# Moving a small tile out of a pool, one load ahead of another, and a last slot in column halves

## The chip, the cores and the metric

The kernel runs on one core of a Trainium2 chip. The metric is the device time of one execution in microseconds (us). Before the change three runs took 1791.95, 1792.40 and 1792.44 us, a median of 1792.4. A run of this kernel can be told from another at about 0.2%, some 3.6 us.

## The reference

Four layers of a streaming encoder on 256 tokens of width 2048, in fp32. Cut to what matters here:

```python
for i in range(DEPTH):                    # 4 layers; kinds 0, 1, 2, 0
    h = rms_norm(x, norm_g[i])
    z = h @ w_in                          # 2048 -> 5632 (kind 0) or 7168 columns (+12 in kind 1)
    mix_out = mixer(z[..., :n_mix])       # gated MLP, forgetting attention or differential attention
    kv = rms_norm(mem, mem_norm_g) @ w_mem_kv[i]      # 2048 -> 1024, 256 memory rows
    mem_out = memory_attention(rms_norm(mem_q), rms_norm(kv[..., :512]), kv[..., 512:])
    branch = concat([mix_out, mem_out], -1) * silu(gate)
    x = x + branch @ w_out[i]             # 2048 -> 2048
```

## The kernel before

**Products.** Nearly all of TensorE's work is the big products: the memory projections of all four layers, the input projections and the output projections. A product is cut into chunks of 512 output columns, a chunk into 8 slots, and a slot takes 256 of the 2048 summed rows: two depth tiles (`kk`) of 128. There are 592 slots in all. Each fp32 operand is split into a rounded part and the rest (`hi` and `lo`), and a product of two operands is three matmuls: hi x hi, lo x hi and hi x lo. So a slot is 2 (`kk`) x 2 (token tiles `t`) x 3 = 12 matmuls of 128x128 stationary against 128x512 moving (lines 170 to 172 in `slot_product`). The stationary tile is a slice of the activations (`bh`/`bl` or `xh`/`xl`, 128 tokens of one depth tile), the moving one a slice of the weights (`whi`/`wlo`). In the last slot of a chunk the first token tile goes first.

**Which activations.** `bh0` to `bh7` with `bl0` to `bl7` hold the memory's transposed rows first (64 slots, before the layers) and later the branch (the output projections, 128 slots). `xh0` to `xh7` with `xl0` to `xl7` hold the token rows for the input projections (400 slots). The number is the slot's share of the depth, `kp`.

**Where the tiles lie.** A tile's place in a partition comes from its pool: pools stand one behind another, and in a pool tiles stand in the order in which they are first asked for. The weight pool `wpool` has only tiles of 4096 bytes. The pool `act` follows: `bh0, bl0, bh1, bl1` (2048 bytes each, asked for in the start-up code), then the three buffers of the row factors `r` (`row_factors`, line 369: 16 columns of which 2 are used, 64 bytes each, 192 bytes in all), then all the other parts `b` and `x`, each 2048 bytes. Within a multiple of 512 bytes the built program has all weight tiles and the parts b0 and b1 at 416, and the parts b2 to b7 and x0 to x7 at 96. A slice of a tile starts a multiple of 512 bytes behind the tile's start. So in the slots of b0 and b1 (48 of the 592) the stationary and the moving operand lie at the same place within 512 bytes, and in the other 544 they lie 192 bytes apart.

**Order of the work.** The order on TensorE, ScalarE (ACT), VectorE (DVE) and SyncE (SP) is that of the code. Between two slots (`between_slots`) the running tasks (norms, attention, gates, residuals) each issue one step, small fp32 products and transposes among them (of PE's 8290 matmul records 7104 are those of the slots and 520 are transposes), and the weights of the slot four ahead are split: ACT copies `raw` to `whi` (line 119), DVE subtracts for `wlo` (line 120). SP loads `raw` up to eight slots ahead.

**Start.** Line 243 loads the first half of the memory tile on ACT's queue, line 244 the norm weights `gk` behind it, and SP's queue loads the first weight tile and the other half. The first split (`scaled_part`, line 205) needs both loads of ACT's queue.

**End.** `residual_task` adds the old rows to an output chunk (line 788, one DVE addition for each token tile). In the last layer the sum goes straight to the output, the first token tile from SP's queue, the second from ACT's (line 790).

Of the kernel before, what the change touches and what calls it, by code (L numbers as in the profile page):

```python
# [9 lines left out]
F32 = mybir.dt.float32  # L10
# [9 lines left out]
P = 128  # L20
D = 2048
S = 256
DEPTH = 4
KT = D // P
CW = 512
# [3 lines left out]
NEG = -1e30  # L29
BIG = 3.0e38  # L30
BIAS_PITCH = 512
ROW_PAD = 16
BIAS_COPIES = 16
RAW_BUFS = 4
PART_BUFS = 4
# [8 lines left out]
def trunk_kernel(  # L44
# [23 lines left out]
    nc = tc.nc  # L68
# [3 lines left out]
    act = ctx.enter_context(tc.tile_pool(name="act", bufs=1))  # L72
    heads = ctx.enter_context(tc.tile_pool(name="heads", bufs=2))
    tmp = ctx.enter_context(tc.tile_pool(name="tmp", bufs=2))
    small = ctx.enter_context(tc.tile_pool(name="small", bufs=32))
# [7 lines left out]
    def piece_sequence():  # L83
        seq = []
        for i in range(1, DEPTH):
            for n in (1, 0):
                seq.append((w_kv[i, n], range(8)))
        for i in range(DEPTH):
            src = (w_a[i // 3], w_b, w_c)[i % 3]
            for n in range(11 if i % 3 == 0 else 14):  # L90
                seq.append((src[n], range(8)))
            for n in range(4):
                seq.append((w_o[i, n], range(8) if n else (0, 1, 2, 3, 6, 7, 4, 5)))
        first = [(w_kv[0, n], kp) for kp in range(8) for n in (1, 0)]
        return first + [(src, kp) for src, order in seq for kp in order]

    pieces = piece_sequence()
# [33 lines left out]
    def tick():  # L131
        for gen in list(tasks):
            if next(gen, tasks) is tasks:
                tasks.remove(gen)
        tasks.extend(fresh)
        fresh.clear()

    def run_late():
        todo = list(late)
        late.clear()  # L140
        for fn in todo:
            fn()

    def between_slots():
        tick()
        split_until(state["slot"] + PART_BUFS)
        load_until(state["slot"] + PART_BUFS + RAW_BUFS)
        run_late()

    def slot_product(acc, parts_of, first, last):  # L150
        between_slots()
        slot = state["slot"]
        kp = pieces[slot][1]
        guard = 0
        while parts_of(kp) is None:
            assert (tasks or fresh) and guard < 100
            tick()
            run_late()
            guard += 1
        xh, xl = parts_of(kp)  # L160
        hi, lo = parts.pop(slot)
        order = [(kk, t) for kk in range(2) for t in range(2)]
        if last:
            order.sort(key=lambda o: o[1])
        for kk, t in order:
            begin, end = first and kk == 0, last and kk == 1
            wh = hi[:, kk * CW : (kk + 1) * CW]
            wl = lo[:, kk * CW : (kk + 1) * CW]
            c = slice(kk * S + t * P, kk * S + (t + 1) * P)
            nc.tensor.matmul(acc[t], xh[:, c], wh, start=begin, stop=False)  # L170
            nc.tensor.matmul(acc[t], xh[:, c], wl, start=False, stop=False)  # L171
            nc.tensor.matmul(acc[t], xl[:, c], wh, start=False, stop=end)  # L172
        state["slot"] += 1
# [4 lines left out]
    def chunk_product(parts_of):  # L178
        acc = new_acc()
        for n in range(8):  # L180
            slot_product(acc, parts_of, n == 0, n == 7)
        return acc

    def pair_product(parts_of):
        accs = [new_acc(), new_acc()]
        for n in range(16):
            slot_product(accs[n % 2], parts_of, n < 2, n >= 14)
        return accs


    gk = const.tile([P, 5 * KT], F32, name="gk")
# [6 lines left out]
    def new_parts(kind, kp):  # L198
        hi = act.tile([P, 2 * S], F32R, tag=f"{kind}h{kp}", name=f"{kind}h{kp}")
        lo = act.tile([P, 2 * S], F32R, tag=f"{kind}l{kp}", name=f"{kind}l{kp}")  # L200
        return hi, lo
# [8 lines left out]
    def scaled_split(hi, lo, src, gcol):  # L210
        for kk in range(2):
            c = slice(kk * S, (kk + 1) * S)
            scaled_part(hi[:, c], lo[:, c], src[:, c], gcol + kk)
# [26 lines left out]
    raw = tmp.tile([P, 2 * S], F32, tag="xo", name="xraw", bufs=4)  # L240
    m_hi, m_lo = new_parts("b", 0)
    bparts[0] = (m_hi, m_lo)
    nc.scalar.dma_start(raw[:, :S], mem_t[0, :, :S])
    nc.scalar.dma_start(gk, gk_in)
    nc.sync.dma_start(w_raw[:, :CW], pieces[0][0][0, :, :CW])
    nc.sync.dma_start(raw[:, S:], mem_t[0, :, S:])
    nc.sync.dma_start(w_raw[:, CW:], pieces[0][0][0, :, CW:])
# [5 lines left out]
    for k in range(2):  # L253
        c, w = slice(k * S, (k + 1) * S), slice(k * CW, (k + 1) * CW)
# [21 lines left out]
    def finish_rms(ss, r):  # L276
        nc.vector.tensor_reduce(r, ss, AX.X, ALU.add)
        rsqrt_mean(r, r, 2, D)
# [88 lines left out]
    mk_d = [dram.tile([P, 4 * S], F32, name=f"mk_d{i}") for i in range(DEPTH)]  # L367
    mv_d = [dram.tile([P, 2 * CW], F32, name=f"mv_d{i}") for i in range(DEPTH)]
    def row_factors(name):
        return act.tile([P, ROW_PAD], F32, tag="r", name=name, bufs=3)[:, :2]  # L370

    r_mem, r_x = row_factors("r_mem"), row_factors("r_x")

    def delayed(n, gen):
# [7 lines left out]
    for i in range(DEPTH):  # L382
        acc = first_accs[0] if i == 0 else chunk_product(lambda kp: bparts[kp])
# [7 lines left out]
        acc = first_accs[1] if i == 0 else chunk_product(lambda kp: bparts[kp])  # L391
# [381 lines left out]
    def old_rows(i, n):  # L773
        res = []
        for t in range(2):
            rows, cols = slice(t * P, (t + 1) * P), slice(n * CW, (n + 1) * CW)
            xo = tmp.tile([P, CW], F32, tag="xo", name="xo", bufs=4)
            nc.sync.dma_start(xo, x[rows, cols] if i == 0 else x_d[i - 1][n][t])
            res.append(xo)
        return res  # L780

    def residual_task(acc, i, n, xo, ss, r_next):
        last = i == DEPTH - 1
        xn = []
        for t in range(2):
            rows, cols = slice(t * P, (t + 1) * P), slice(n * CW, (n + 1) * CW)
            xt = tmp.tile([P, CW], F32, tag="tb", name="xn", bufs=4)
            nc.vector.tensor_add(xt, acc[t], xo[t])  # L788
            if last:
                (nc.sync, nc.scalar)[t].dma_start(out[rows, cols], xt)  # L790
                continue
            nc.gpsimd.dma_start(x_d[i][n][t], xt)  # L792
            xn.append(xt)
        if last:
            return

        def squares():
            for t in range(2):
                sq = tmp.tile([P, CW], F32, tag="sq", name="sq", bufs=2)
                nc.scalar.activation(sq, xn[t], AF.Square, accum_out=ss[:, t, n : n + 1])  # L800

        late.append(squares)
        for jj in range(2):
            yield
            kp = 2 * n + jj
            tb = ps_t.tile([P, 4, P], F32, tag="t", name="tb")
            for kk in range(2):
                for t in range(2):
                    f = (2 * jj + kk) * P
                    nc.tensor.transpose(tb[:, 2 * kk + t, :], xn[t][:, f : f + P], ident)  # L810
            hi, lo = new_parts("x", kp)
            scaled_split(hi, lo, tb.rearrange("p a b -> p (a b)"), KT * (i + 1) + 2 * kp)
            xparts[kp] = (hi, lo)
        if n == 3:
            finish_rms(ss, r_next)

    for i in range(DEPTH):
# [9 lines left out]
        def product():  # L827
            return chunk_product(lambda kp: xparts[kp])
# [26 lines left out]
        if kind == 0:  # L855
# [3 lines left out]
            for c in range(3):  # L859
                acc = product()  # L860
# [9 lines left out]
            for c in range(3):  # L870
                acc = product()
# [6 lines left out]
        else:  # L878
# [10 lines left out]
            for c in range(3):  # L889
                ready = []  # L890
                acc = product()
                qt = heads.tile([P, 4, S], F32, tag="qT", name="qt")
                spawn(norm_task(acc, r_x, qgains[:, gq : gq + 1], width, qt))
                acc = product()
# [11 lines left out]
                acc = product()  # L906
# [22 lines left out]
            for c in range(3):  # L929
                gate(c)  # L930

        r_next = row_factors("r_x")
        ss = small.tile([P, 2, 4], F32, tag="ss", name="ss", bufs=2)
        for n in range(4):
            xo = old_rows(i, n)
            acc = chunk_product(lambda kp: bnext[kp])
            spawn(residual_task(acc, i, n, xo, ss, r_next))
# [89 lines left out]
```

## Time and profile before

| | before |
|---|---|
| runs (3) | 1791.95 to 1792.44 us, median 1792.4 |
| profiled execution | 1792.09 us |
| its span, first to last instruction | 1790.3 us |
| TensorE (PE) busy | 1782.3 us, 8290 matmul records |
| weight loads (PEld) busy | 1461.0 us |
| VectorE busy | 1021.0 us |
| ScalarE busy | 905.1 us |
| granted TensorE clock, mean | 1.000 |

A busy matmul record overlaps the next one: of a stream of equal matmuls the time is read from the distance between starts, not from the records' length. The profiled execution is 1.8 us longer than its span, and 0.3 us under the median of the runs.

### The profile page before, as it was taken

What the parts mean: (1) busy time and instruction counts of PE and PEld (TensorE: products, weight loads), DVE (VectorE), ACT (ScalarE), POOL (GpSimd) and SP (SyncE); (2) the same over time, 40 slices, a digit from 0 to 9 for tenths busy, and PEclk for the clock granted to TensorE, in tenths of its full rate; (3) what the DMA queues carried; (4) which work ended last, traced back from release to release, by engine and by line L of the source; (5) the groups of instructions that cost most, each with busy time, mean ns of one, the idle gap of its engine ahead of it and who ended that gap; (6) DMA issues with size and microseconds to landing.
All of it is one profiled execution on the core that took longest, in us unless ns stands there. A gap on an engine that the chain in (4) does not pass through costs nothing.

```text
span 1790.3 us, 22226 instructions
## 1 busy us (share of the span) xinstructions
PE 1782.3 (100%) x8290; PEld 1461.0 (82%) x8290; DVE 1021.0 (57%) x1431; ACT 905.1 (51%) x1273; POOL 115.5 (6%) x138
## 2 busy tenths in 40 slices
PE   9999999999999999999999999999999999999999
PEld 6788888888888888888888887878788888888887
DVE  5555557555555555555555555666565556755453
ACT  6555545544555544545445555565554544554432
POOL 0110100000001101010000110102000000100000
PEclk9999999999999999999999999999999999999999
DMA  8767765555676554455767655454546766455564
GB/s 297 268 229 259 245 225 169 188 178 183 225 227 197 173 193 153 160 182 170 206 221 228 198 174 171 156 167 169 172 157 219 230 217 229 157 172 180 188 219 158
DMA packets 103452, 353.91 MB, mean 198 GB/s; under 512 B 12028, under 2 KB 12340, under 8 KB 103216
## 3 DMA queue, kind: packets, MB, share of 16 engines
q1 hardware_dynamic: 97200, 332.84, 56.2%
q0 software_dynamic: 5280, 18.44, 3.3%
q8 instruction: 65, 1.06, 0.3%
q10 hardware_dynamic: 864, 1.22, 0.2%
q14 instruction: 43, 0.35, 0.1%
HBM read 339.55 MB, written 12.89 MB: 197 GB/s over the span
## 4 chain that ended last, share of the span: by engine, by line
PE 96%; DMA 2%; ACT 0%; DVE 0%; issue 0%; POOL 0%; SPq 0%; ACTq 0%; DVEq 0%; POOLq 0%
PE acc L170 30%; PE acc L172 29%; PE acc L171 29%; PE tb L562 2%; PE tb L357 1%; PE tb L571 1%; PE tb L622 1%; PE s L470 1%; PE s L512 1%; DMA row<-in_mem_dram 1%; PE sv L688 1%; DMA raw<-in_w_kv_dram 1%; PE tb L810 1%; PE s L487 0%; DMA mv_d<-mvv 0%; DMA xraw<-in_mem_t_dram 0%
## 5 line engine op out<-in xcount | busy, mean ns | idle before, releaser
L120 DVE TENSOR_TENSOR wlo<-raw,whi 128x1024 fp32r<-128x1024 f32 x591 | 722.8, 1224 | 604.9 <-ACT whi L119 600.7
L119 ACT CAST whi<-raw 128x1024 fp32r<-128x1024 f32 x591 | 619.3, 1049 | 523.9 <-PE acc L172 470.1
L170 PE MATMUL acc<-whi,xh 128*128 128x512 f32 x1600 | 646.3, 404 | 0.0
L172 PE MATMUL acc<-whi,xl 128*128 128x512 f32 x1600 | 628.2, 393 | 0.0
L171 PE MATMUL acc<-wlo,xh 128*128 128x512 f32 x1600 | 623.8, 390 | 0.0
L172 PEld LDWEIGHTS acc<-whi,xl 128*128 128x128 f32 x1600 | 300.4, 188 | 68.8
L170 PEld LDWEIGHTS acc<-whi,xh 128*128 128x128 f32 x1600 | 300.9, 188 | 63.9 <-issue 3.2
L171 PEld LDWEIGHTS acc<-wlo,xh 128*128 128x128 f32 x1600 | 301.0, 188 | 61.3
L170 PE MATMUL acc<-whi,bh 128*128 128x512 f32 x768 | 304.3, 396 | 1.3 <-ACT whi L256 0.7
L171 PE MATMUL acc<-wlo,bh 128*128 128x512 f32 x768 | 300.4, 391 | 0.8 <-DVE wlo L120 0.6
L172 PE MATMUL acc<-whi,bl 128*128 128x512 f32 x768 | 300.2, 391 | 0.0
L172 PEld LDWEIGHTS acc<-whi,bl 128*128 128x128 f32 x768 | 144.2, 188 | 32.6 <-DVE bl L206 0.4
L170 PEld LDWEIGHTS acc<-whi,bh 128*128 128x128 f32 x768 | 144.3, 188 | 32.2 <-ACT whi L256 1.3
L171 PEld LDWEIGHTS acc<-wlo,bh 128*128 128x128 f32 x768 | 144.4, 188 | 32.0 <-DVE wlo L120 1.7
L575 ACT COPY pt<-tb 128x256 f32<-128x256 f32 (+1 forms) x80 | 27.2, 341 | 127.4 <-PE tb L571 127.3
L320 POOL TENSOR_TENSOR sc<-sc,expo 128x8 f32<-128x8 f32 (+1 forms) x23 | 55.9, 2431 | 540.3 <-DVE sc L319 474.0
L206 DVE SCALAR_TENSOR_TENSOR xl<-tb,gk,xh 128x256 fp32r<-128x256 f32 x48 | 23.2, 484 | 29.6 <-ACT xh L205 29.5
L205 ACT ACTIVATE xh<-tb,gk 128x256 fp32r<-128x256 f32 x48 | 22.8, 475 | 33.0 <-PE tb L810 19.7
L626 ACT CAST bh<-tb 128x512 fp32r<-128x512 f32 x26 | 15.3, 588 | 47.4 <-PE tb L622 47.4
L792 POOL DMA_DIRECT2D x_d<-xn x24 | 13.2, 549 | 314.1 <-DVE xn L788 313.3
L475 DVE TENSOR_REDUCE st<-s 128x1 f32<-128x256 f32 x32 | 13.6, 425 | 32.2 <-PE s L470 32.2
L585 DVE TENSOR_SCALAR mo<-tb,st 128x128 f32<-128x128 f32 x56 | 19.4, 346 | 19.3 <-ACT pt L575 16.5
(160 smaller groups left out, 959.6 us busy)
## 6 DMA issues: line engine op xcount, KB each, us to landing
raw<-in_w_a_dram SPq DMA_DIRECT2D x176, 512.0 KB, 3.3
raw<-in_w_o_dram SPq DMA_DIRECT2D x128, 512.0 KB, 3.6
raw<-in_w_b_dram SPq DMA_DIRECT2D x112, 512.0 KB, 3.3
raw<-in_w_c_dram SPq DMA_DIRECT2D x112, 512.0 KB, 3.2
raw<-in_w_kv_dram SPq DMA_DIRECT2D x63, 512.0 KB, 4.3
x_d<-xn POOLq DMA_DIRECT2D x24, 256.0 KB, 6.1
xo<-x_d SPq DMA_DIRECT2D x24, 256.0 KB, 5.5
lnp<-in_ln_dram SPq DMA_DIRECT2D x12, 256.0 KB, 6.1
```

Source lines behind the costliest of these rows:

```text
L119: nc.scalar.copy(hi, raw)
L120: nc.vector.tensor_sub(lo, raw, hi.bitcast(F32))
L170: nc.tensor.matmul(acc[t], xh[:, c], wh, start=begin, stop=False)
L171: nc.tensor.matmul(acc[t], xh[:, c], wl, start=False, stop=False)
L172: nc.tensor.matmul(acc[t], xl[:, c], wh, start=False, stop=end)
L205: nc.scalar.activation(hi, src, AF.Copy, scale=g)
L206: nc.vector.scalar_tensor_tensor(lo, src, g, hi.bitcast(F32), ALU.mult, ALU.subtract)
L320: nc.gpsimd.tensor_tensor(sc[:, :, :n], sc[:, :, :n], expo.rearrange("p (a b) -> p a b", a=2)[:, :, :n], ALU.pow,)
L357: nc.tensor.transpose(tb[:, i, :], qn[t][:, i * P : (i + 1) * P], ident)
L562: nc.tensor.matmul(av, pt[:, j * P : (j + 1) * P], vv[:, j, f], start=(j == 0), stop=(j == tiles(t) - 1),)
L575: nc.scalar.copy(pt[:, : nk * P], tb[:, : nk * P])
L585: nc.vector.tensor_scalar(mo[t][:, f], av, done_st[:, 2:3], None, ALU.mult)
```

## The change

Four edits. The row factors are no longer tiles of the `act` pool but of `small`, the last of the pools there, with 2 columns; with that every part `b` and `x` lies at 416 within 512 bytes, as the weight tiles do, and everything that stands behind the old `r` tiles moves down by 192 bytes (the constants, among them `ident`, stay). The load of `gk` is issued ahead of that of the memory tile. The very last slot is issued by `final_slot`: 24 matmuls of 256 moving columns, token tile by token tile, left column half first. And in the last layer the residual addition and the store of each token tile are made in two column halves, the left one stored from SP's queue, the right one from ACT's.

```diff
--- before.py
+++ after.py
@@ -29,7 +29,6 @@
 NEG = -1e30
 BIG = 3.0e38
 BIAS_PITCH = 512
-ROW_PAD = 16
 BIAS_COPIES = 16
 RAW_BUFS = 4
 PART_BUFS = 4
@@ -147,6 +146,19 @@
         load_until(state["slot"] + PART_BUFS + RAW_BUFS)
         run_late()
 
+    def final_slot(acc, xh, xl, hi, lo):
+        half = CW // 2
+        for t in range(2):
+            for a in (0, half):
+                for kk in range(2):
+                    w = slice(kk * CW + a, kk * CW + a + half)
+                    c = slice(kk * S + t * P, kk * S + (t + 1) * P)
+                    for n, (xx, ww) in enumerate(((xh, hi), (xh, lo), (xl, hi))):
+                        nc.tensor.matmul(
+                            acc[t][:, a : a + half], xx[:, c], ww[:, w],
+                            start=False, stop=(a > 0 and kk == 1 and n == 2),
+                        )
+
     def slot_product(acc, parts_of, first, last):
         between_slots()
         slot = state["slot"]
@@ -159,6 +171,9 @@
             guard += 1
         xh, xl = parts_of(kp)
         hi, lo = parts.pop(slot)
+        if slot == len(pieces) - 1:
+            final_slot(acc, xh, xl, hi, lo)
+            return
         order = [(kk, t) for kk in range(2) for t in range(2)]
         if last:
             order.sort(key=lambda o: o[1])
@@ -240,8 +255,8 @@
     raw = tmp.tile([P, 2 * S], F32, tag="xo", name="xraw", bufs=4)
     m_hi, m_lo = new_parts("b", 0)
     bparts[0] = (m_hi, m_lo)
+    nc.scalar.dma_start(gk, gk_in)
     nc.scalar.dma_start(raw[:, :S], mem_t[0, :, :S])
-    nc.scalar.dma_start(gk, gk_in)
     nc.sync.dma_start(w_raw[:, :CW], pieces[0][0][0, :, :CW])
     nc.sync.dma_start(raw[:, S:], mem_t[0, :, S:])
     nc.sync.dma_start(w_raw[:, CW:], pieces[0][0][0, :, CW:])
@@ -367,7 +382,7 @@
     mk_d = [dram.tile([P, 4 * S], F32, name=f"mk_d{i}") for i in range(DEPTH)]
     mv_d = [dram.tile([P, 2 * CW], F32, name=f"mv_d{i}") for i in range(DEPTH)]
     def row_factors(name):
-        return act.tile([P, ROW_PAD], F32, tag="r", name=name, bufs=3)[:, :2]
+        return small.tile([P, 2], F32, tag="r", name=name, bufs=3)
 
     r_mem, r_x = row_factors("r_mem"), row_factors("r_x")
 
@@ -785,10 +800,15 @@
         for t in range(2):
             rows, cols = slice(t * P, (t + 1) * P), slice(n * CW, (n + 1) * CW)
             xt = tmp.tile([P, CW], F32, tag="tb", name="xn", bufs=4)
+            if last:
+                for a in (0, CW // 2):
+                    w = slice(a, a + CW // 2)
+                    nc.vector.tensor_add(xt[:, w], acc[t][:, w], xo[t][:, w])
+                    (nc.sync, nc.scalar)[a > 0].dma_start(
+                        out[rows, cols.start + w.start : cols.start + w.stop], xt[:, w]
+                    )
+                continue
             nc.vector.tensor_add(xt, acc[t], xo[t])
-            if last:
-                (nc.sync, nc.scalar)[t].dma_start(out[rows, cols], xt)
-                continue
             nc.gpsimd.dma_start(x_d[i][n][t], xt)
             xn.append(xt)
         if last:
```

The order of the instructions differs in three places. On ACT the two loads at the start of the program (`xraw` is the memory tile's half) stood so before:

```order
L243 DMA xraw<-in_mem_t_dram 128x256
L244 DMA gk<-in_gk_dram 128x80
L250 ACT_TABLE_LOAD
L250 CAST warm_act<-warm 128x1 [waits DVE_49]
L205 ACTIVATE bh_94<-xraw,gk 128x256 [waits DMAHW2_49,DMAHW0_49]
```

and stand so now:

```order
L258 DMA gk<-in_gk_dram 128x80
L259 DMA xraw<-in_mem_t_dram 128x256
L265 ACT_TABLE_LOAD
L265 CAST warm_act<-warm 128x1 [waits DVE_49]
L220 ACTIVATE bh_94<-xraw,gk 128x256 [waits DMAHW2_49,DMAHW0_49]
```

The two loads have changed places, and the first split waits for both as it did. On PE the end of the last slot, the second token tile, was this (`acc_14446` is its accumulator, `bh_13681` and `bl_13682` are b7):

```order
L170 MATMUL acc_14446<-whi,bh_13681 128x512
L171 MATMUL acc_14446<-wlo,bh_13681 128x512
L172 MATMUL acc_14446<-whi,bl_13682 128x512
L170 MATMUL acc_14446<-whi,bh_13681 128x512
L171 MATMUL acc_14446<-wlo,bh_13681 128x512
L172 MATMUL acc_14446<-whi,bl_13682 128x512
```

and is this now (`acc_14458`; the first six rows are the left half, the last six the right one):

```order
L157 MATMUL acc_14458<-whi,bh_13681 128x256
L157 MATMUL acc_14458<-wlo,bh_13681 128x256
L157 MATMUL acc_14458<-whi,bl_13682 128x256
L157 MATMUL acc_14458<-whi,bh_13681 128x256
L157 MATMUL acc_14458<-wlo,bh_13681 128x256
L157 MATMUL acc_14458<-whi,bl_13682 128x256
L157 MATMUL acc_14458<-whi,bh_13681 128x256
L157 MATMUL acc_14458<-wlo,bh_13681 128x256
L157 MATMUL acc_14458<-whi,bl_13682 128x256
L157 MATMUL acc_14458<-whi,bh_13681 128x256
L157 MATMUL acc_14458<-wlo,bh_13681 128x256
L157 MATMUL acc_14458<-whi,bl_13682 128x256
```

Each matmul with its weight load has become two, so the slot has 24 pairs where it had 12; no other matmul of the program has moved. On DVE the last additions of the program were these:

```order
L120 TENSOR_TENSOR wlo<-raw,whi 128x1024 [waits DMAHW6_49,Activation_49]
L788 TENSOR_TENSOR xn<-acc_14445,xo 128x512 [waits DMAHW4_49,PE_49]
L788 TENSOR_TENSOR xn<-acc_14446,xo 128x512 [waits DMAHW5_49,PE_49]
```

and are these now:

```order
L119 TENSOR_TENSOR wlo<-raw,whi 128x1024 [waits DMAHW4_49,Activation_49]
L806 TENSOR_TENSOR xn<-acc_14457,xo 128x256 [waits DMAHW2_49,PE_49]
L806 TENSOR_TENSOR xn<-acc_14457,xo 128x256
L806 TENSOR_TENSOR xn<-acc_14458,xo 128x256 [waits DMAHW3_49,PE_49]
L806 TENSOR_TENSOR xn<-acc_14458,xo 128x256
```

Each addition has become two, and of a token tile only the left half waits for PE: the count it waits for is the one that the last matmul of the whole token tile sets, the right half's included.

## Rows read from the trace of the kernel before

**Rows 1.** Busy time by stretch: PE, PEld, DVE, ACT, POOL, PEclk, DMA share, GB/s
```profile
20.00:60.00 40.00, 39.28 (x170) 31.05 (x169) 22.70 (x30) 26.73 (x45) 1.33 (x2) 1.00 0.83 289
...
1000.00:1780.00 780.00, 780.00 (x3639) 638.59 (x3638) 456.33 (x695) 391.67 (x560) 43.14 (x40) 1.00 0.56 187
```
**Rows 2.** Waits of PE, longest first: us in total, times, longest
```profile
PE warm_ps L252 <- DVE warm L249: 1.2, 1, 1.2
```
**Rows 3.** Timeline of PE, last chunk (start us, us): first matmuls of b0, b2 and b7
```profile
1763.81 0.39 PE L170 MATMUL acc<-whi,bh 128*128 128x512 f32 x1
...
1769.25 0.39 PE L170 MATMUL acc<-whi,bh 128*128 128x512 f32 x1
...
1782.98 0.39 PE L170 MATMUL acc<-whi,bh 128*128 128x512 f32 x1
```
**Rows 4.** Timeline of PE, layer 3: transposes, x3 first and last, x4, x1
```profile
1636.24 0.60 PE L622 MATMUL tb<-ident,br 128*128 128x128 f32 x4
1636.60 0.48 PE L170 MATMUL acc<-whi,xh 128*128 128x512 f32 x1
...
1639.21 0.39 PE L172 MATMUL acc<-whi,xl 128*128 128x512 f32 x1
1639.44 0.39 PE L170 MATMUL acc<-whi,xh 128*128 128x512 f32 x1
...
1653.17 0.39 PE L170 MATMUL acc<-whi,xh 128*128 128x512 f32 x1
```
**Rows 5.** Timeline of PE, a slot of b1 behind transposes, first and last matmul
```profile
520.98 0.49 PE L810 MATMUL tb<-ident,xn 128*128 128x128 f32 x3
521.23 0.48 PE L170 MATMUL acc<-whi,bh 128*128 128x512 f32 x1
...
523.84 0.39 PE L172 MATMUL acc<-whi,bl 128*128 128x512 f32 x1
```
**Rows 6.** Timeline of PE: eight small fp32 products in a row, next slot behind
```profile
1606.51 1.05 PE L688 MATMUL sv<-v,ws 128*128 128x128 f32 x8
1607.32 0.48 PE L170 MATMUL acc<-whi,xh 128*128 128x512 f32 x1
```
**Rows 7.** Timeline of ACT, start: issue of `gk`; first split and what ended its wait
```profile
1.19 0.45 ACTq L244 DMA_DIRECT2D gk<-in_gk_dram  x1
...
4.99 0.51 ACT L205 ACTIVATE bh<-xraw,gk 128x256 fp32r<-128x256 f32 x1 [1.84 <-DMA gk<-in_gk_dram]
```
**Rows 8.** DMA issues, first 14 us: count, KB each, us to landing
```profile
raw<-in_w_kv_dram SPq DMA_DIRECT2D x2, 256.0 KB, 3.6
...
xraw<-in_mem_t_dram ACTq DMA_DIRECT2D x1, 128.0 KB, 3.7
...
gk<-in_gk_dram ACTq DMA_DIRECT2D x1, 40.0 KB, 3.7
```
**Rows 9.** Timeline of ACT: the last of four splits that wait for loads
```profile
14.13 1.05 ACT L119 CAST whi<-raw 128x1024 fp32r<-128x1024 f32 x1 [0.95 <-DMA raw<-in_w_kv_dram]
```
**Rows 10.** Timeline of PE: products of 128x256 against 12 stationary columns
```profile
624.05 0.28 PE L725 MATMUL z<-xh,fh 128*12 128x256 f32 x1
624.17 0.28 PE L726 MATMUL z<-xl,fh 128*12 128x256 f32 x1
```
**Rows 11.** Timeline of PE: fp32 product of 128x256 in two passes, next slot behind
```profile
291.43 0.60 PE L470 MATMUL s<-mk,mqt 128*128 128x256 f32 x2
291.68 0.58 PE L170 MATMUL acc<-whi,xh 128*128 128x512 f32 x1
```
**Rows 12.** Timeline, end of the program: last matmul, last addition, last store
```profile
1785.50 0.39 PE L172 MATMUL acc<-whi,bl 128*128 128x512 f32 x1
1785.92 0.69 DVE L788 TENSOR_TENSOR xn<-acc,xo 128x512 f32<-128x512 f32 x1 [0.68 <-PE acc L172]
1786.65 0.34 ACTq L790 DMA_DIRECT2D out_dram<-xn  x1
```
**Rows 13.** Timeline of DVE: two operations of 256 columns, back to back
```profile
9.57 0.87 DVE L206 SCALAR_TENSOR_TENSOR bl<-xraw,gk,bh 128x256 fp32r<-128x256 f32 x2
```

## The prediction

> **What bounds the kernel now.** I read the table by stretch first. From 1000 to 1780 us PE is busy for all 780.00 us, VectorE and ScalarE for little more than half, the DMA share is 0.56 and the granted clock 1.00, so TensorE is at its upper level of 2.4 GHz [rows 1]. The list of waits comes next: the longest that PE has in the whole program is 1.2 us, before its first matmul [rows 2]. Busy records overlap, so neither view says what one matmul costs. For that I read the timeline and take distances between starts. The end of the kernel is thus set by the sum of TensorE's steps, some 7100 of them for the products, and one nanosecond on each is 7 us. Only the first 65 us or so are different: there the DMA share is 0.83, and PE still works 39.28 of 40 us [rows 1].
>
> **The place of the parts.** In the kernel before, b0 and b1 lie where the weights lie within 512 bytes, the other parts 192 bytes off; so its trace holds both cases. In the last chunk the slots b0 and b1 take 1769.25 - 1763.81 = 5.44 us, 2.720 each. The five slots b2 to b6 right behind them take 1782.98 - 1769.25 = 13.73 us, 2.746 each [rows 3]. Same engine, same clock, same weights queue, same accumulators: 0.026 us a slot, or 2.2 ns on each of 12 steps (0.019 to 0.033 by the rounding of the starts). The token parts are at the distant place too, and five of their slots in a row take 1653.17 - 1639.44 = 13.73 us, the same 2.746 [rows 4]. Nothing in the kernel before has an x part at the weights' place, so that x behaves as b does there is inferred, from its equal time at the other place.
>
> Not every slot is so undisturbed. Behind a burst of small products or transposes the first steps of a slot are late, whatever its parts. Slot x3 behind four transposes takes 1639.21 - 1636.60 = 2.61 us from its first matmul to its twelfth [rows 4]; a slot of b1 behind transposes takes 523.84 - 521.23 = 2.61 us [rows 5]. To the hundredth they are equal. With two rounded differences the gain of such a slot lies between 0 and 0.02 us; I take the middle, 0.01.
>
> Along the whole timeline 544 slots are at the distant place (400 of x, 144 of b), 193 of them (170 and 23) start right behind such a burst, and 351 do not. Of the 351 some 14 run in the first 65 us, where loads set the pace, and I give them nothing. So:
> - 337 undisturbed slots x 0.026 us = 8.8 us, bounds 6.4 and 11.1;
> - 193 slots behind a burst x 0.01 = 1.9 us, bounds 0 and 3.9.
>
> Together 10.7 us off, between 6.4 and 15.0. What is late next when PE's steps shorten? A slot's feed is one split of 1.05 us on ScalarE [rows 9] and one on VectorE, beside a slot of 2.72 us, and the DMA share would rise from 0.56 by a hundredth of itself [rows 1]; none of these comes near.
>
> The rule that speaks against this edit is in the Trainium skill, "TensorE: Matmul & The Clock Gate", section "Part 2: What happens when you issue a matmul": TensorE has one SBUF read port for the moving operand and another for the weight load, independent of each other, so loading the next weights takes no read bandwidth from the running matmul. By that rule the place of one operand against the other should not matter, and the sum would be 0 instead of 10.7. The rows above disagree: the two places differ by 1% of a slot, in neighbouring slots [rows 3].
>
> **The small products.** Their own tiles all lie behind the old row factors and move together, so among themselves nothing changes. Only those that read `ident`, a constant that stays, get a new distance: the transposes, 520 records. From the first of four to the next slot they take 1636.60 - 1636.24 = 0.36 us [rows 4], from the first of three 521.23 - 520.98 = 0.25 [rows 5]: 0.11 a step, and 0.03 for the last one, into the slot. Eight small products at one common place take 1607.32 - 1606.51 = 0.81 us [rows 6], without the last step 0.111 each. The two kinds of distance step alike to some 0.004 us by the rounding. I take 0, with bounds of 2 us (520 x 0.004) on both sides.
>
> **The norm weights first.** The first split starts at 4.99 us and has waited for `gk` [rows 7]. `gk` landed 3.7 us after its issue, and so did the memory half issued ahead of it [rows 8]; an issue takes 0.45 us of the queue [rows 7]. The split needs both. With the order turned, `gk` lands early and the larger load takes the place of the last one on the same queue: the wait passes from one to the other. I take 0, with 0.45 us as the best case (the larger load lands as soon as it did) and -0.4 as the worst (it is held up by as much). What it gains is moreover exposed to what follows: the split at 14.13 waits for a weight load again [rows 9], and that load was issued only when an early split had released a buffer, so a part of any shift would carry through.
>
> **The last slot.** 24 matmuls of 256 columns replace 12 of 512. The trace has 256-column products of this kind only with 12 stationary columns: 0.115 us a step, start to start [rows 10]. With 128 stationary columns it has an fp32 product of 256 columns, two records that with the short step of 0.03 into the next slot fill 0.25 us, 0.22 for one record [rows 11]. So the slot takes between 24 x 0.115 = 2.76 and 24 x 0.22 = 5.3 us, where it took 2.75. I take the lower end, as the nearest row has the slot's own operand type: 0.0, at worst 2.5 us more.
>
> **The tail.** The last addition starts at 1785.92, 0.42 after the last matmul, takes 0.69, and its store is issued at 1786.65 [rows 12]. Now both halves wait for the last matmul of the token tile, since PE signals only there. Two operations of 256 columns back to back take 0.87 us on VectorE [rows 13], so the right half's store is issued 0.18 us later than now. It carries half the bytes; but at the start a load of 256 KB landed 3.6 us after its issue and one of 128 KB 3.7 [rows 8], so the bytes saved show no time there. The span's last 3.65 us [rows 12] stay. I take 0, from 0.2 us more (nothing gained by the smaller store) to 0.4 less (half of the store's transfer gained). In the three earlier chunks of the last layer VectorE makes twice as many additions and SP's queue waits one addition longer before the next loads of old rows and weights; SP runs up to eight slots ahead, some 20 us, which hides it. Without that cover it would cost 0.2 us a chunk.
>
> **The sum.** 1792.09 for the profiled execution, minus 10.7, is 1781.4; the runs' median is 0.3 above that execution, so 1781.7 us.
>
> **Rivals.**
> - *Place does not matter for TensorE, and b0 and b1 are fast for a reason of their own*. For it: b0 and b1 are also the first two slots of a chunk. Against it: the stretch of x holds x0, the first slot of a chunk, and no slot time below 2.746 on average [rows 4]. Nothing else gains: 1792.4. Chance 6%. (The Trainium skill's two ports for TensorE's reads would bring this.)
> - *Only the b parts gain.* The x slots have never been seen at the near place. 121 undisturbed slots of b x 0.026 + 23 x 0.01 = 3.4 us: 1789.0. Against it: x and b take 2.746 at the distant place. Chance 4%.
> - *The slots behind a burst gain in full*, since there too both operands' distance is gone: 530 x 0.026 = 13.8 us: 1778.6. Against it: the b1 slot behind transposes shows 2.61 as x3 does [rows 4, 5]. Chance 7%.
> - *Crowding at the one place: slower.* After the change what ScalarE writes (`whi`), VectorE writes (`wlo`) and TensorE reads twice lie at one place within 512 bytes in every slot. If the late steps behind a burst come from such meetings, they would spread: 544 slots that each lose what a disturbed slot has over an undisturbed one. Eleven undisturbed steps are 11/12 of 2.746 = 2.517, with a first step that is longer by what the burst's last step lacks (0.11 - 0.03 = 0.08) 2.597; 2.61 is 0.013 more. 544 x 0.013 = 7.1 us: 1799.5. It decides from the point at which less than a third of the slots keep the 0.026. Against it: in the undisturbed slots of b0 and b1 both splits run too, and they take 2.720. Chance 4%.
> - The forecast, with the place at work as the slots of b0 and b1 show it: 79%.
>
> **How the numbers follow.** The forecast's own bounds run from 15.0 off with 2 gained on the transposes and 0.4 at each end of the program, 1774.6, to 6.4 off with 2 lost on the transposes, 2.5 in the last slot, 0.4 at the start and 0.2 in the tail, 1791.1; so many ends seldom meet, and its own range is 1778.5 to 1785.5. The range that should hold 8 in 10 takes a little of the full-gain rival below and of a partial gain above: 1777.8 to 1786.5. This kernel's runs tell a change from none at about 0.2%, 3.6 us. Faster by more: the forecast 79%, the full gain 7%, and half of the b-only case 2%, 88%. Same: the two-port case 6% and the other half 2%, 8%. Slower 4%.
>
> **What would show it.** In the changed kernel's timeline an undisturbed slot of x, and of b2 to b7, takes 2.72 us instead of 2.746; that is the step on which nearly all rests, and x slots still at 2.746 would make the forecast wrong. A slot behind transposes stays near 2.61 from first to twelfth matmul. The first split begins within 0.4 us of 4.99 and waits for the memory tile, not for `gk`. The 24 half matmuls step by about 0.115; steps near 0.2 would cost 2 us. Between the last matmul's start and the span's end there are 4.8 us now, and about as many after.

## The result, and the profile after

The changed kernel takes 1781.47 us (median of 4 runs, 1781.33 to 1781.52) against 1792.18 before (4 runs, 1790.84 to 1792.44): a ratio of 0.9942, 95% interval 0.9924 to 0.9959. It is 10.7 us faster. The forecast was 1781.7.

| | before | after |
|---|---|---|
| profiled execution, us | 1792.09 | 1781.33 |
| its span, us | 1790.3 | 1779.6 |
| PE busy, us | 1782.3 | 1771.4 |
| PE, matmul records | 8290 | 8302 |
| mean granted clock | 1.000 | 1.000 |

One row of the table by stretch of the changed kernel (columns as in [rows 1]):

```profile
1000.00:1770.00 770.00, 770.00 (x3617) 634.12 (x3616) 453.60 (x699) 389.76 (x558) 45.14 (x40) 1.00 0.56 187
```

PE is as full as before and at the same granted clock, 1.00, but there are more matmuls in the same time: 3617 in 770 us are 4.70 per us, where 3639 in 780 us were 4.67. The gain is in the step, the distance from the start of one matmul to the start of the next. The timeline of PE in the last chunk, the first matmul of b2 and the first of the last slot:

```profile
1758.54 0.39 PE L185 MATMUL acc<-whi,bh 128*128 128x512 f32 x1
...
1772.14 0.28 PE L157 MATMUL acc<-whi,bh 128*128 128x256 f32 x1
```

Five slots, b2 to b6, take 13.60 us, 2.720 each; the same five took 13.73 [rows 3]. The token parts do the same. The timeline of PE at the place of [rows 4]: four transposes, slot x3 behind them from its first matmul to its twelfth, then the first of x4, and of x1 five slots on:

```profile
1626.50 0.60 PE L637 MATMUL tb<-ident,br 128*128 128x128 f32 x4
1626.86 0.47 PE L185 MATMUL acc<-whi,xh 128*128 128x512 f32 x1
...
1629.46 0.39 PE L187 MATMUL acc<-whi,xl 128*128 128x512 f32 x1
1629.68 0.39 PE L185 MATMUL acc<-whi,xh 128*128 128x512 f32 x1
...
1643.29 0.39 PE L185 MATMUL acc<-whi,xh 128*128 128x512 f32 x1
```

Five undisturbed slots, x4 to x0, take 13.61 us where they took 13.73. Slot x3 behind the burst takes 2.60 us to its twelfth matmul, where it took 2.61 [rows 4]. The four transposes, with the step into the slot, take 0.36 us as before.

The start, ACT's timeline (the first split as in [rows 7], the split of [rows 9]):

```profile
4.75 0.51 ACT L220 ACTIVATE bh<-xraw,gk 128x256 fp32r<-128x256 f32 x1 [1.59 <-DMA xraw<-in_mem_t_dram]
...
14.10 1.05 ACT L118 CAST whi<-raw 128x1024 fp32r<-128x1024 f32 x1 [0.94 <-DMA raw<-in_w_kv_dram]
```

The first split comes 0.24 us earlier and now waits for the memory tile instead of `gk`. By the split at 14.10 only 0.03 of it is left, and then nothing. The timeline of PE where the memory projections' first keys are transposed, in the kernel before:

```profile
64.56 0.66 PE L357 MATMUL tb<-ident,qn 128*128 128x128 f32 x4 [0.34 <-DVE qn L334]
```

and in the changed kernel:

```profile
64.58 0.66 PE L372 MATMUL tb<-ident,qn 128*128 128x128 f32 x4 [0.88 <-DVE qn L349]
```

Both reach it at the same time, and PE in the changed kernel has waited 0.88 us for it, not 0.34: in the first 65 us PE's saving turned into a wait, as the forecast had taken it. The end of the program:

```profile
1774.78 0.28 PE L157 MATMUL acc<-wlo,bh 128*128 128x256 f32 x1
1774.90 0.28 PE L157 MATMUL acc<-whi,bl 128*128 128x256 f32 x1
1775.21 0.76 DVE L806 TENSOR_TENSOR xn<-acc,xo 128x256 f32<-128x256 f32 x2 [0.68 <-PE acc L157]
...
1776.00 0.34 ACTq L807 DMA_DIRECT2D out_dram<-xn  x1
```

The half matmuls step by 0.12 us. From the first start to the last start of the last slot there are 1774.90 - 1772.14 = 2.76 us, where there were 1785.50 - 1782.98 = 2.52 [rows 3, 12]. From the last start to the span's end there are 4.7, where there were 4.8 [rows 12]: the addition starts 0.31 us behind the last start instead of 0.42, the last store (of the right half) is issued 0.79 us behind the addition's start instead of 0.73, and from its issue to the end of the span it is 3.6 us instead of 3.65.

So the 10.7 us by which the span is shorter are, from front to back: 0.02 lost up to the first keys; from there to the last slot 1718.42 us before and 1707.56 after, 10.86 gained; 0.24 lost in the last slot; some 0.1 gained in the tail.

### The profile page after: what moved, and what is told of

It reads as the page before. It is cut to its first block, busy times and chain, and to the rows that moved or that the text cites. A ratio compares the mean times of both kernels' runs of the same rounds, so it can differ in the third digit from the quotient of the medians.

```text
span 1779.6 us, 22276 instructions
## 1 busy us (share of the span) xinstructions
PE 1771.4 (100%) x8302; PEld 1461.0 (82%) x8302; DVE 1020.7 (57%) x1439; ACT 905.4 (51%) x1273; POOL 117.4 (7%) x138
## 4 chain that ended last, share of the span: by engine, by line
PE 96%; DMA 2%; ACT 0%; DVE 0%; issue 0%; POOL 0%; SPq 0%; ACTq 0%; DVEq 0%; POOLq 0%
PE acc L185 30%; PE acc L187 29%; PE acc L186 29%; PE tb L577 2%; DMA xraw<-in_mem_t_dram 1%; PE tb L372 1%; PE tb L586 1%; PE tb L637 1%; PE s L485 1%; PE s L527 1%; DMA raw<-in_w_kv_dram 1%; PE sv L703 1%; PE tb L830 1%; DMA mv_d<-mvv 0%; PE s L502 0%; ACT whi L118 0%
## 5 line engine op out<-in xcount | busy, mean ns | idle before, releaser
L185 PE MATMUL acc<-whi,bh 128*128 128x512 f32 x764 | 300.7, 394 | 1.1 <-ACT bh L220 0.7
```

## The experiments

The theory was that the distance between stationary and moving operand sets TensorE's step. The rivals were that the other edits bring a part, that the stationary operand's own place counts, and that another distance is as good. A fourth, that the stationary operand's place matters against what other engines read and write beside the weights, is settled below by stretches in which no other engine works.

**The move alone.**

```diff
 (the kernel before)
     def row_factors(name):
-        return act.tile([P, ROW_PAD], F32, tag="r", name=name, bufs=3)[:, :2]
+        return small.tile([P, 2], F32, tag="r", name=name, bufs=3)
```

> The kernel before with the row factors moved out of the pool, and nothing else. Theory (the distance of stationary and moving operand within 512 bytes sets TensorE's step): all of the gain, 1781 to 1782 us, undisturbed slots at 2.720 us. Rival (a part of the gain is from the load order, the last slot or the halved stores): clearly above the changed kernel, 1783 or more.

1781.00 us (4 runs, 1780.89 to 1781.80), ratio to the kernel before 0.9941 (0.9926 to 0.9956). Five slots, b2 to b6 of the last chunk, take 13.60 us. As far as these runs can tell, the move is the whole gain.

**All but the move.**

```diff
 (the changed kernel)
+ROW_PAD = 16
 ...
     def row_factors(name):
-        return small.tile([P, 2], F32, tag="r", name=name, bufs=3)
+        return act.tile([P, ROW_PAD], F32, tag="r", name=name, bufs=3)[:, :2]
```

> The changed kernel with the row factors back in their old pool, so that the parts b2 to b7 and x lie 192 bytes off again; early load of the norm weights, last slot and stores in halves are kept. Theory: no gain, 1791.5 to 1792.7 us, undisturbed slots of x at 2.746 us. Rival (the other three edits bring a part): 1790 or less.

1792.27 us (10 runs, 1790.96 to 1793.37), ratio 1.0002 (0.9993 to 1.0012). PE's timeline, first matmul of b2 and of the last slot:

```profile
1769.92 0.39 PE L186 MATMUL acc<-whi,bh 128*128 128x512 f32 x1
...
1783.65 0.28 PE L158 MATMUL acc<-whi,bh 128*128 128x256 f32 x1
```

Five slots are back at 13.73 us. The early load, the last slot in halves and the stores in halves together make no difference that these runs can tell.

**Weights and parts moved together.**

```diff
 (the changed kernel)
     gk = const.tile([P, 5 * KT], F32, name="gk")
+    const.tile([P, 48], F32, name="shift")
```

> The changed kernel with a tile of 192 bytes that nothing uses, ahead of the first tile: weights, parts and all that follows move by 192 bytes together and now lie at 96 within 512, the place where the parts were when they were slow. Theory (the distance counts): as the changed kernel, 1781 to 1782 us, slots at 2.720. Rival (the stationary operand's own place counts, 416 being fast and 96 slow): slots at 2.746, 1791 to 1793 us.

1780.88 us (4 runs, 1780.25 to 1781.92), ratio 0.9938 (0.9922 to 0.9955). PE's timeline, the same two places:

```profile
1759.11 0.39 PE L185 MATMUL acc<-whi,bh 128*128 128x512 f32 x1
...
1772.71 0.28 PE L157 MATMUL acc<-whi,bh 128*128 128x256 f32 x1
```

13.60 us. The parts lie where they lay when they were slow, at 96 within 512, and are fast, since the weights lie there too. The stationary operand's own place is out as the cause.

Other engines are out as well. Weights are split four slots ahead, so in the last chunk slots b5 and b6 run with PE alone at work. The table by stretch for these two slots (columns as in [rows 1]), in the kernel before:

```profile
1777.49:1782.98 5.49, 5.49 (x26) 4.51 (x24) 0.00 (x0) 0.00 (x0) 0.00 (x0) 1.00 0.00 0
```

and with the parts 128 bytes off the weights, a run of the next experiment:

```profile
1801.47:1807.08 5.61, 5.61 (x26) 4.51 (x25) 0.00 (x0) 0.00 (x0) 0.00 (x0) 1.00 0.00 0
```

VectorE, ScalarE, GpSimd and the DMA share are at 0.00, and the two slots still take 5.49 and 5.61 us; in the changed kernel they take 5.44 (1766.70 to 1772.14), also with nothing beside them. So what counts is the distance between PE's own two operands.

**The distance.** Nine kernels are the changed kernel with an unused tile of N bytes ahead of all parts, so that b0 to b7 and x0 to x7 lie N bytes off the weights; what stands behind the parts moves along. For 256:

```diff
 (the changed kernel)
+    act.tile([P, 64], F32, tag="shift", name="shift")
+
     def new_parts(kind, kp):
```

and for the others 8, 16, 24, 32, 40, 48, 56 and 80 columns of 4 bytes. What was expected, in the order in which they ran:

> The changed kernel with a tile of 256 bytes that nothing uses, ahead of the parts: all parts lie 256 bytes off the weights. Theory as the change has it (same place within 512 bytes): undisturbed slots at 2.746, the 48 slots of b0 and b1 too, 1792 to 1794 us. Rival (same place within 256 bytes is enough): 2.720 and 1781 to 1782 us.

> All parts 128 bytes off the weights (a tile of 128 bytes that nothing uses, ahead of the parts of the changed kernel). 0 and 256 gave undisturbed slots of 2.720 us, 192 gave 2.747. If the pattern repeats every 128 bytes: 2.720 and 1781 us. If every 256, 128 is a distance like any other: 2.74 or more, 1790 to 1794 us.

> All parts 64 bytes off the weights. If the pattern repeats every 128 bytes, 64 is what 192 was: 2.747 a slot and 1791 to 1793 us, the slots of b0 and b1 slow as well. If it repeats every 256 and is worst half way, less than 2.747. If every 64 bytes were the same, 192 would have been fast: so 2.720 here would mean that the distance itself does not decide.

> All parts 32 bytes off the weights. If what counts is equal or unequal: 2.747 a slot, 1791 to 1793 us. If the cost grows with the distance from the nearest equal place: between 2.720 and 2.747, 1783 to 1790 us.

> All parts 96 bytes off the weights. As for 32 bytes: 2.747 if only equal or unequal counts; between if the cost grows with the distance from the nearest equal place, and then as 32 bytes if the pattern repeats every 128 (96 is 32 short of it), and more than 32 bytes if every 256.

> All parts 224 bytes off the weights, 32 short of 256. So far an undisturbed slot took 2.720 us at 0 and 256, 2.747 at 192 (in the kernel before), 2.800 at 32, 64 and 128, 2.812 at 96. If the cost falls towards 256: between 2.720 and 2.747 a slot, 1782 to 1792 us. If 0 is not the best place but only a good one: under 2.720 and under 1780 us, which would beat both kernels. If every unequal place is as bad as 32: 2.800, 1818 us.

> All parts 160 bytes off the weights, between 128 (2.800 us a slot) and 192 (2.747). If the cost falls steadily from 128 on: 2.77 to 2.78 a slot, 1800 to 1810 us. If it has only two levels: 2.747 or 2.800.

> All parts 320 bytes off the weights, which is 64 within 256. If the pattern repeats every 256 bytes: 2.800 a slot and 1818 us, as at 64. If it repeats every 512 and is the same to both sides of the weights' place: 320 is as 192 on the other side, 2.747 and 1792 to 1794 us. If 0 and 256 are merely two good places: anything.

> All parts 192 bytes off the weights, b0 and b1 too: the distance that 544 slots of the kernel before have, by an unused tile ahead of all parts and with the other three edits kept. If the distance alone makes the slot, undisturbed slots of all parts take 2.747 us, and the time is the kernel before's plus 48 slots of at most 0.027, 1792 to 1793.5 us. If 192 is as its neighbours 160 and 224 (2.800), and the slots of the kernel before are faster for another reason (b0 and b1 at the near place, or what lies behind the parts): 2.800 and some 1819 us.

Measured, with the slot as a fifth of b2 to b6 in the last chunk:

| distance, bytes | five slots, us | one slot, us | time, us |
|---|---|---|---|
| 0 (the changed kernel) | 13.60 | 2.720 | 1781.47 |
| 256 | 13.60 | 2.720 | 1781.91 (4 runs) |
| 192 | 13.73 | 2.746 | 1792.31 (10 runs) |
| 32 | 14.00 | 2.800 | 1818.28 (1 run) |
| 64 | 14.00 | 2.800 | 1818.47 (1 run) |
| 128 | 14.00 | 2.800 | 1816.28 (1 run) |
| 160 | 14.00 | 2.800 | 1819.13 (1 run) |
| 224 | 14.00 | 2.800 | 1819.04 (4 runs) |
| 320 | 14.00 | 2.800 | 1820.09 (1 run) |
| 96 | 14.06 | 2.812 | 1825.63 (1 run) |

The kernel before ran beside them at 1792.63 (32, 64, 96 and 128) and at medians of 1791.44 (256), 1791.73 (160, 224 and 320) and 1791.90 (192). A single run gives its time without a spread, but each of them lies more than 23 us above the kernel before, and the five slots agree with it. The rows of three of them, PE's timeline at the same two places; at 256:

```profile
1758.77 0.39 PE L185 MATMUL acc<-whi,bh 128*128 128x512 f32 x1
...
1772.37 0.28 PE L157 MATMUL acc<-whi,bh 128*128 128x256 f32 x1
```

at 128:

```profile
1793.08 0.40 PE L185 MATMUL acc<-whi,bh 128*128 128x512 f32 x1
...
1807.08 0.28 PE L157 MATMUL acc<-whi,bh 128*128 128x256 f32 x1
```

and at 192:

```profile
1769.83 0.39 PE L185 MATMUL acc<-whi,bh 128*128 128x512 f32 x1
...
1783.56 0.28 PE L157 MATMUL acc<-whi,bh 128*128 128x256 f32 x1
```

What matters is the difference of the two times in each pair: 13.60, 14.00 and 13.73 us for the same sixty matmuls.

What follows. The same place within 256 bytes is enough; the theory in the change's own words, 512, asked for too much, and of the two answers expected for 256 the rival's came. Every other distance tried costs, and mostly far more than the one that the kernel before happened to have. At 128, 64 and 32 the expectations had named times of at most 1794 us, and at 96 a slot of at most 2.747 us; all four missed, the times by 22 us or more. Nor does the cost fall towards 256: 224 is as bad as 32 (ratio 1.0154, 1.0137 to 1.0170), though the expectation had left room there for a time under both kernels. The run at 320 has the slot of 64, and of most other distances, and not that of 192: a pattern that repeats only every 512 bytes and is the same to both sides is out. That 192 costs less than its neighbours 160 and 224 is no accident of the kernel before: made anew, with b0 and b1 at it too, it gives 2.746 again. Why 192 is so, and 96 a little worse than the rest, no run here settles.

One thing more lies in the same traces. The last slot, of 256-column matmuls, ranks the distances otherwise. PE's timeline at 64, the first and the last matmul of that slot:

```profile
1809.39 0.28 PE L157 MATMUL acc<-whi,bh 128*128 128x256 f32 x1
...
1812.01 0.28 PE L157 MATMUL acc<-whi,bl 128*128 128x256 f32 x1
```

From first to last start it takes 2.62 us at 64 and at 320, a step of 0.114 us, but 2.75 to 2.76 at 0 and 256, a step of 0.12; at 192 it takes 2.71, at 160 2.76, and elsewhere something between. That 64 and 320 agree, and 0 and 256, again fits a pattern that repeats every 256 bytes. But "0 is best" is shown for 512 columns only; with 256 it is nearly the worst of the distances tried. That rests on one slot of each run.

## Why the prediction was right

**The place of the parts.** Right, in mechanism and size. The forecast took 2.720 a slot from b0 and b1 and gave it to all; that x would follow was inferred, and x does. 337 undisturbed slots x 0.026 were to give 8.8 us and those behind a burst 1.9, 10.7 together; the stretch from the first keys to the last slot gained 10.86. Added up slot by slot over both timelines, without the first 24 slots, the slots (b0 and b1 among them) with no burst before them gained 9.2 us and those behind one 1.4. Both terms were a little off, in opposite directions, so that the sum met the measurement to 0.2 us is in part luck. A slot of x behind a burst gained 0.008 us on average, where 0.01 had been taken as the middle of what the rounding left open; x3 went from 2.61 to 2.60. The full-gain rival is out, and why these slots gain so little is not explained.

The rule of the Trainium skill that spoke against the edit ("TensorE: Matmul & The Clock Gate", section "Part 2: What happens when you issue a matmul": the weight load's read port is independent of the moving operand's, so loading takes nothing from the running matmul) gives no reason for a difference, and by it the scan of distances would be flat. The traces disagree: 2.720 to 2.812 us a slot by the distance alone. Which part of the chip the two operands share is not shown.

**The rivals.** That b0 and b1 were fast for a reason of their own, and that only b gains, fell with the x slots. Crowding at one place, the slower case, fell with them too: with everything at one place the undisturbed slots of x and of b take 2.720.

**The first 65 us.** Right that 14 slots there give nothing: the first keys are reached at 64.58 instead of 64.56, behind a longer wait.

**The norm weights first.** Right to be taken at 0. The wait passed to the memory tile as described; the 0.24 us gained was inside the bounds and gone by the next waits for loads.

**The last slot.** The step was mis-sized a little: 0.12 us, not 0.115 (the two starts in [rows 10] read 0.12 as they stand). So the slot takes 24 x 0.12 = 2.88 us instead of 2.75, 0.13 lost where nothing was expected. The 0.24 us read above from first to last start is the same loss and 0.11 more, since the last of 24 starts lies nearer to its slot's end than the last of 12; that 0.11 comes back in the tail. The bound of 2.5 was far off; halves of 256 columns with their own weight loads do run at about half the step of 512.

**The tail.** Taken at 0, measured some 0.1 us gained, for reasons that the forecast did not have. The addition starts 0.31 us behind the last matmul's start instead of 0.42, as the last matmul's record is shorter by as much, 0.28 us instead of 0.39. The second addition costs less than bounded: the pair takes 0.76 us, not 0.87, and the last store is issued 0.06 us later, not 0.18. From the last store's issue to the end of the span there are 3.63 and 3.66 us in the two runs with whole stores and 3.56 to 3.61 in the twelve with halves, so the smaller store brings a little.

**The small products.** Taken at 0: the four transposes still take 0.36 us though their distance to `ident` has changed by 192 bytes.

## What to carry to other kernels

Where a stream of matmuls is the bound, look at the addresses of stationary and moving tiles, not only at their shapes: three buffers of 64 bytes in the pool of the operands shifted every operand behind them, and here the distance alone was worth up to 2.5% of the kernel (1781.47 to 1825.63 us). The busy share and the waits do not show it; the distance between the starts of equal matmuls does, and a kernel whose tiles lie at two distances already holds the experiment in its own trace. Keep tiles whose size is no multiple of 256 bytes out of the pools that hold operands, or behind the operands. Which distance is best was measured here for one kind of matmul, 128x512 with its own weight load; for another width, measure again.

## What the runs showed of the hardware that was not expected

- The step of a 128x512 matmul with its own 128x128 weight load, both of the split fp32 kind, depends on the distance of the two operands, with no other engine at work too: 2.720 us for twelve (226.7 ns each) at 0 and 256 bytes, 2.746 (228.8) at 192, 2.800 (233.3) at 32, 64, 128, 160, 224 and 320, 2.812 (234.3) at 96, all at a granted clock of 1.00.
- The same kind with 256 columns steps by 0.12 us at 0 and 256 bytes and by 0.114 at 64 and 320, the other way round than with 512 columns (one slot in each run).
- A slot behind a burst of transposes stays late whether the distance is good or not: from first to twelfth matmul x3 took 2.61 and 2.60 us, where eleven steps of an undisturbed slot are 2.52 and 2.49.
